# A hybrid decoder step: head sums and gate products on parts of the TensorE array, inverses on partitions 0 to 63

## The chip, the cores and the metric

The kernel runs on one core of a Trainium2 chip. The metric is the device time of one execution in microseconds (us). The core's engines work side by side, each through its own instructions in order: TensorE (PE, with its weight loads PEld), VectorE (DVE), ScalarE (ACT), GpSimd (POOL) and SyncE (SP). SP and POOL issue the DMAs here. On-chip memory has 128 partitions; matrix products go to eight PSUM banks.

## What is computed

One inference step of one decoder layer, in float32, for a new sequence of 1024 tokens and for 8 running sequences with 4 tokens each ("sampled rows", 32 in all). Two branches read the same projection `z = x @ w_in`; they are gated, merged, projected and followed by a SwiGLU network. What the change touches lies in the two branches:

```python
# RWKV-7 branch
w = -softplus(-(w0 + tanh(w_lo) @ w2)) - 0.5 ; decay = exp(-exp(w))   # w_lo: 64 columns
a = sigmoid(a0 + a_lo @ a2)                                           # a_lo: 64 columns
kk = k * k_k                                                          # 16 heads of 64 channels
kk = kk / max(sqrt(sum(kk * kk, over the head)), 1e-12)
# scan over tokens, state S (64 x 64) for each head
sa = S @ -kk ; S = S * decay + sa (x) (kk * a) + v (x) k ; y = S @ r
# RG-LRU branch: u is a causal convolution of width 4; 16 blocks of 64 channels
r = sigmoid(u_block @ wa_block + ba) ; i = sigmoid(u_block @ wi_block + bi)
a = exp(-8 * r * softplus(-lam)) ; h_t = a * h_(t-1) + sqrt(1 - a*a) * i * u
```

## The kernel before, in words

**Two parts.** The first, some 1300 us, is the mixing part: the projections of `x` and both branches. The second is the output projection's rest, the layer norms and the SwiGLU network, mostly dense products. The change touches the first, and prices that the planner uses in both.

**Tiling.** Channels lie on partitions, tokens along the free dimension. The 1024 channels are 8 tiles of 128, which is two heads each; a unit `u` is a pair of tiles (`i` = 0, 1) in one half of the sequence (`p`): 4 pairs x 2 halves = 8 units, so 16 channel tiles in all. A row of a tile is 576 columns (`W`): for p = 0 the sampled rows at 28 to 60 (`SO` to `ZO`) and 512 tokens from 64 (`PO`); for p = 1 the tokens alone. A PSUM bank holds 512 float32 columns, so `pieces(p)` cuts p = 0 into 292 and 256 columns and leaves p = 1 whole at 512.

**Projections.** `gemm_tile`, called by the main task, multiplies each weight tile with `x` as three fp32r products (high and low parts). They are recorded at line 246.

**Background tasks.** All else runs in Python generators that issue into a list; the recorded line of their instructions is 316, and matmuls of one task are told apart by tile names. A planner (`Ticker`, with a `Clock` that prices each instruction) decides the whole order before the kernel is built: between two projection matmuls it takes the first instruction of a background task that would be ready by its clock, lower `prio` first. A matmul of a task is taken once its inputs are 0.6 us old by that clock. The order on every engine is then fixed; at run time each instruction waits until its inputs are really there. `Clock.cost` holds durations, `Clock.op` what order adds: for PE 0.094 us where the part of the array changes.

**The RWKV branch.** For each tile, `wkv_tile` computes:

- the two gates with `bg_mm`, which takes a PSUM bank of the three in `Bk`, runs its list of matmuls and hands the bank to ACT. The weights `w2` and `a2` have 64 rows each; `lora` stores them over 128 rows, the other half zero, and `wa` holds `w_lo` and `a_lo` on partitions 0 to 63 and 64 to 127. Each gate is three fp32r products (`parts3`);
- the head sums: `sel` (128 x 128, two columns used) times the squares in `t6`, a float32 product, of which two rows are copied by ACT and written by four small DMAs to `ssd` in DRAM, from where `wkv` reads them as `n2`.

`stage` then copies two groups of four 64-token chunks (`g` = 0, 1) into `arm` and `bk`, and `inverse(u, g, n2)` inverts triangular matrices: float32 products of `bk` and `arm` on row halves of the array; a DMA through DRAM to `bn`; a loop of 15 steps with two small DVE instructions each on `bn`, `bt` and `btmp`, on partitions `64 * g` to `64 * g + 63`; DMAs through `bte`, `bze` and DRAM into `tdv` and `zt`; then small products on 32 x 32 quarters that DVE and ACT instructions on `zt`, `tdv` and `nz` join. `chain` carries the state over the 8 chunks of a unit: product `cx`, copies to `xs`, product `cu`, copies to `su`, product `cs_`, four updates on DVE. Each copy is made in two halves, one by ACT and one by DVE.

**The RG-LRU branch.** `lru` (lowest priority) computes the convolution `ut`, then each gate as one float32 product with a 128 x 128 weight that holds two 64 x 64 blocks on its diagonal, then activations, a scan and the products.

**Sampled rows.** `sample` handles them for p = 0. Its state update `ps2` is a pair of float32 products on two 64 x 64 quarters of the array, one from each row half, into one bank.

Of the kernel before, what the change touches and what calls it, by code (L numbers as in the profile page):

```python
# [37 lines left out]
C_ID, C_MP, C_SCAN, C_MS, C_MX, C_MB, C_SEL, C_BONES, C_M16, C_N = 0, 128, 256, 768, 832, 896, 904, 1032, 1160, 1161  # L38
# [38 lines left out]
class Clock:  # L77
# [6 lines left out]
    def __init__(self):  # L84
        self.t = dict.fromkeys(("PE", "ACT", "DVE", "POOL", "SP", "DMA"), 0.0)
        self.uses = {}
        self.masks = {}
        self.table = 0
        self.tile = None
        self.port = {"DVE": [], "POOL": []}  # L90
# [86 lines left out]
    def op(self, e, f, args, kw, at, last):  # L177
# [8 lines left out]
        else:  # L186
            if e == "PE":
# [4 lines left out]
                self.tile = tile  # L192
            lock = False
# [152 lines left out]
def tile_hybrid_step(ctx: ExitStack, tc: tile.TileContext, I, O):  # L346
# [131 lines left out]
    with ExitStack() as zctx:  # L478
# [69 lines left out]
        lora = [T(f"lora{i}", [128, 2, 2, 128], F32R) for i in range(2)]  # L548
# [41 lines left out]
        sel = cst[:, C_SEL:C_SEL + 128]  # L590
# [10 lines left out]
        for x in lora:  # L601
            pool.memset(x.bitcast(F32), 0.0)
# [89 lines left out]
        def load2(dst, src, flag, after):  # L692
# [5 lines left out]
            if len(dst[0].shape) == 3:  # L698
                split2([x.rearrange("p i m -> p (i m)") for x in dst], t[:, 0:256])
            else:  # L700
                for n in range(2):
                    b = slice(64 * n, 64 * n + 64)
                    split2([x[b, n].rearrange("p i m -> p (i m)") for x in dst], t[b, 0:256])
# [4 lines left out]
        def bg_mm(p, ops, use):  # L708

            for t0, t1 in pieces(p):  # L710
# [5 lines left out]
                Bk.put(ps)  # L716
            yield
# [10 lines left out]
        def wkv_tile(u, i, parts, side):  # L728
# [13 lines left out]
            t4 = yield from temps.take()  # L742
            yield from bg_mm(p, parts3([x[:, 1, i] for x in lora], wa),
                             lambda a, b, ps: A(t4[:, a:b], ps[:, :b - a], AF.Tanh, 0.5, D(D_A0H, q)))
# [1216 lines left out]
```

## Time and profile before

| | us |
|---|---|
| median of three runs | 2140.77 (2139.39 to 2144.16) |
| the profiled execution | 2158.58 |
| its span, first to last instruction | 2156.8 |
| mean granted TensorE clock | 0.962 |

The span is divided by the profile into busy time of each engine; a group of instructions is named by line, engine, operation and "written tile<-read tiles", with rows*columns of the array that a matmul uses, then the moving operand's shape. A float32 product is recorded as two matmuls. `bank` is any PSUM bank, `tmp` any of the 15 rows of scratch. PE's lengths include the way to PSUM, so neighbours overlap, and the distance from start to start tells what one costs.

### The profile page before, as it was taken

What the parts mean: (1) busy time and instruction counts of PE and PEld (TensorE: products, weight loads), DVE (VectorE), ACT (ScalarE), POOL (GpSimd) and SP (SyncE); (2) the same over time, 40 slices, a digit from 0 to 9 for tenths busy, and PEclk for the clock granted to TensorE, in tenths of its full rate; (3) what the DMA queues carried; (4) which work ended last, traced back from release to release, by engine and by line L of the source; (5) the groups of instructions that cost most, each with busy time, mean ns of one, the idle gap of its engine ahead of it and who ended that gap; (6) DMA issues with size and microseconds to landing.
All of it is one profiled execution on the core that took longest, in us unless ns stands there. A gap on an engine that the chain in (4) does not pass through costs nothing.

```text
span 2156.8 us, 44027 instructions
## 1 busy us (share of the span) xinstructions
PE 2065.4 (96%) x17664; PEld 1792.2 (83%) x17664; DVE 1226.6 (57%) x2967; ACT 1070.5 (50%) x2475; POOL 389.2 (18%) x797
## 2 busy tenths in 40 slices
PE   7799999999999999999999899999999999999997
PEld 7788898897986777777777697889999999999987
DVE  5676695796877887777867666522322322222226
ACT  4656756757666677767576735821121122112221
POOL 1101210220310310211212020221211211111124
PEclk9897997999999999999999799999999999999999
DMA  4131231131241231232313323221111211111112
GB/s 137 56 92 36 66 95 48 51 107 51 76 131 60 78 97 52 67 86 67 98 58 90 113 96 133 88 69 38 61 40 35 64 40 47 37 54 49 40 50 81
DMA packets 124925, 152.85 MB, mean 71 GB/s; under 512 B 82784, under 2 KB 87296, under 8 KB 124720
## 3 DMA queue, kind: packets, MB, share of 16 engines
q0 software_dynamic: 31936, 112.75, 15.6%
q1 hardware_dynamic: 92784, 37.28, 7.0%
q8 instruction: 139, 2.28, 0.4%
q14 instruction: 66, 0.54, 0.1%
HBM read 132.45 MB, written 17.57 MB: 70 GB/s over the span
## 4 chain that ended last, share of the span: by engine, by line
PE 76%; DVE 10%; ACT 9%; issue 3%; DMA 1%; POOL 0%; SPq 0%; DVEq 0%; ACTq 0%; POOLq 0%
PE bank L246 60%; PE bank L316 15%; DVE tmp L316 2%; DVE wl L316 1%; ACT tmp L316 1%; ACT wh L316 1%; DVE su L316 1%; ACT L316 1%; ACT arm L316 1%; ACT nz L316 1%; ACT bk L316 1%; DVE btmp L316 1%; DVE bt L316 1%; DVE arm L316 1%; DVE rge L316 1%
## 5 line engine op out<-in xcount | busy, mean ns | idle before, releaser
L246 PE MATMUL bank<-xx,wh 128*128 128x512 f32 (+4 forms) x3168 | 808.3, 342 | 26.9 <-ACT xx L246 8.5
L246 PEld LDWEIGHTS bank<-xx,wh 128*128 128x128 f32 x3168 | 553.5, 196 | 88.7 <-ACT xx L246 8.5
L246 PE MATMUL bank<-xx,wl 128*128 128x512 f32 (+4 forms) x1584 | 541.3, 342 | 0.0
L316 DVE TENSOR_TENSOR wl<-wraw,wh 128x512 fp32r<-128x512 f32 (+2 forms) x336 | 264.3, 788 | 264.2 <-ACT wh L316 262.1
L316 ACT ACTIVATE wh<-wraw 128x512 fp32r<-128x512 f32 (+2 forms) x408 | 246.1, 610 | 274.6 <-PE bank L246 245.6
L246 PE MATMUL bank<-hl,wh 128*128 128x272 f32 (+1 forms) x1056 | 342.6, 324 | 0.9 <-DVE hl L316 0.9
L246 PE MATMUL bank<-hh,wh 128*128 128x272 f32 (+1 forms) x1056 | 341.1, 323 | 0.5 <-ACT hh L316 0.5
L246 PE MATMUL bank<-hh,wl 128*128 128x272 f32 (+1 forms) x1056 | 341.5, 323 | 0.0
L246 PEld LDWEIGHTS bank<-xx,wl 128*128 128x128 f32 x1584 | 310.6, 196 | 28.3 <-issue 3.0
L246 PEld LDWEIGHTS bank<-hh,wh 128*128 128x128 f32 x1056 | 198.7, 188 | 17.3 <-ACT hh L316 1.2
L246 PEld LDWEIGHTS bank<-hl,wh 128*128 128x128 f32 x1056 | 198.7, 188 | 17.2 <-DVE hl L316 1.5
L246 PEld LDWEIGHTS bank<-hh,wl 128*128 128x128 f32 x1056 | 198.6, 188 | 15.3
L316 POOL DMA_DIRECT2D wraw<-in_win x114 | 61.9, 543 | 782.8 <-DVE wl L316 469.1
L316 POOL TENSOR_TENSOR wl<-wraw,wh 128x512 fp32r<-128x512 f32 (+1 forms) x72 | 86.1, 1196 | 513.3 <-ACT wh L316 490.5
L246 PE MATMUL bank<-u,wh 128*128 128x272 f32 (+1 forms) x768 | 176.7, 324 | 0.0
L246 PEld LDWEIGHTS bank<-u,wh 128*128 128x128 f32 x768 | 128.6, 188 | 11.3
L316 DVE TENSOR_TENSOR acc<-acc,bank 128x272 f32<-128x272 f32 (+3 forms) x96 | 49.9, 519 | 148.2 <-PE bank L246 148.2
L316 ACT ACTIVATE sg<-bank 128x272 f32<-128x272 f32 (+1 forms) x66 | 30.8, 466 | 196.1 <-PE bank L246 196.0
L246 PE MATMUL bank<-u,wl 128*128 128x272 f32 (+1 forms) x384 | 124.3, 324 | 0.0
L316 DVE TENSOR_TENSOR sg<-sg,bank 128x272 f32<-128x272 f32 (+1 forms) x66 | 34.3, 520 | 156.1 <-PE bank L246 156.1
L316 ACT ACTIVATE su<-bank 64x256 f32<-64x256 f32 (+1 forms) x192 | 60.2, 337 | 64.6 <-PE bank L316 62.4
L316 ACT ACTIVATE u<-sg 128x272 fp32r<-128x272 f32 (+1 forms) x66 | 33.1, 502 | 112.1 <-DVE sg L316 112.1
(248 smaller groups left out, 3204.2 us busy)
## 6 DMA issues: line engine op xcount, KB each, us to landing
wraw<-in_win POOLq DMA_DIRECT2D x116, 512.0 KB, 3.6
wraw<-in_wgu POOLq DMA_DIRECT2D x48, 512.0 KB, 3.5
wraw<-in_wo POOLq DMA_DIRECT2D x16, 512.0 KB, 3.6
wraw<-in_wdn POOLq DMA_DIRECT2D x16, 384.0 KB, 3.4
wraw<-in_wdn POOLq DMA_DIRECT2D x16, 320.0 KB, 3.2
mgd<-yb POOLq DMA_DIRECT2D x32, 128.0 KB, 2.7
out_y<-tmp SPq DMA_DIRECT2D x8, 512.0 KB
scrN<-nz SPq DMA_DIRECT2D x64, 32.0 KB
```

Source lines behind the costliest of these rows:

```text
L246: fn(*args, **kw)
L316: fn(*args, **kw)
```

## The change

It has six parts.

1. The decay and the in-context gate of a tile go side by side: `lora` now has 64 rows of each weight without zeros, and the new `pair_mm` takes two banks and issues the two gates' matmuls alternately, one on rows 0 to 63 of the array, one on rows 64 to 127. `load2` splits the weights in one instruction for all partitions, and the start of the kernel no longer clears `lora`.
2. The two gates of the RG-LRU branch: four products of 64 x 64 blocks, on four quarters of the array. Two quarters need `u` on the other half of the partitions, which two DMAs from SBUF to SBUF write into `b`, the tile that later receives the gate. The weights are stored without the zero blocks.
3. The head sums: the 512 token columns are cut into four of 128, each a product with 32 columns of `sel` on its own strip of 32 array columns and into its own 32 partitions. One copy by ACT of 128 columns takes the place of one or two of up to 512. Still four DMAs, now of two chunks each.
4. `bn`, `bt`, `btmp`, `n2` have 64 partitions and a buffer for each `g`; `bte` and `bze` have 64 partitions and serve both.
5. In `chain`, DVE now copies the lower halves and ACT the upper ones, and the four state updates go head by head.
6. The planner: prices for the new products, and 0.12 us where an ACT or DVE instruction starts at another partition than the one before it.

```diff
@@ Clock.cost, Clock.op
             if args[1].dtype == F32R:
-                return max(0.11, n / 2250)
+                return max(0.11, n / 2250) / (128 // k)
             if k <= 32:
-                return 0.045
+                return 0.045 if n == 32 else 0.024 if k == 32 else 0.017
+            if m < 128 and n > 96:
+
+                return n / 600 / min(4, 128 // k * (128 // m))
...
+            if e in ("ACT", "DVE"):
+
+                part = out.offset // out.ap[0][0]
+                at = max(at, self.t[e] + 0.12 * (self.part.get(e, part) != part))
+                self.part[e] = part
@@ tiles
-        lora = [T(f"lora{i}", [128, 2, 2, 128], F32R) for i in range(2)]
+        lora = [T(f"lora{i}", [128, 2, 128], F32R) for i in range(2)]
...
-        bn, bt, btmp = T("bn", [128, 16, 16]), T("bt", [128, 16, 16]), T("btmp", [128, 64])
-        bte, bze = T("bte", [128, 16, 32]), T("bze", [128, 16, 32])
-        n2s = [T(f"n2_{i}", [128, 16]) for i in range(2)]
+        bns, bts, btmps = [[T(f"{n}{g}", [64, *d]) for g in range(2)]
+                           for n, d in (("bn", (16, 16)), ("bt", (16, 16)), ("btmp", (64,)))]
+        bte, bze = T("bte", [64, 16, 32]), T("bze", [64, 16, 32])
+        n2s = [T(f"n2_{i}", [64, 2, 16]) for i in range(2)]
@@ new
+        def pair_mm(p, ops, use_a, use_b):
+
+
+            for t0, t1 in pieces(p):
+                while len(Bk.free) < 2:
+                    yield
+                pa, pb = Bk.get(), Bk.get()
+                for n, group in enumerate(zip(*ops)):
+                    for ps, (lhsT, rhs, *out) in zip((pa, pb), group):
+                        for w, x, o in ((lhsT, rhs, slice(0, 128)),) if not out else zip(lhsT, rhs, out[0]):
+                            MM(ps[o, :t1 - t0], w, x[:, t0:t1], start=n == 0, stop=n == len(ops[0]) - 1)
+                yield
+                use_a(t0, t1, pa)
+                Bk.put(pa)
+                use_b(t0, t1, pb)
+                Bk.put(pb)
+            yield
@@ wkv_tile
-            yield from bg_mm(p, parts3([x[:, 0, i] for x in lora], wa),
-                             lambda a, b, ps: A(t1[:, a:b], ps[:, :b - a], AF.Tanh, 0.5, D(D_W0H, q)))
+            t4 = yield from temps.take()
+            yield from pair_mm(p, [[(a[s, i], b[s]) for a, b in parts3(lora, wa)] for s in (slice(0, 64), slice(64, 128))],
+                               lambda a, b, ps: A(t1[:, a:b], ps[:, :b - a], AF.Tanh, 0.5, D(D_W0H, q)),
+                               lambda a, b, ps: A(t4[:, a:b], ps[:, :b - a], AF.Tanh, 0.5, D(D_A0H, q)))
...
-            yield from bg_mm(p, [(sel, t6)], lambda a, b, ps: A(t6[0:2, a:b], ps[0:2, :b - a]))
...
+            ps = yield from Bk.take()
+            for x in range(4):
+                MM(ps[32 * x:32 * x + 32, 0:128], sel, t6[:, PO + 128 * x:PO + 128 * x + 128], start=True, stop=True)
+            if p == 0:
+                MM(ps[0:32, 128:160], sel, t6[:, SO:ZO], start=True, stop=True)
+            yield
+            A(t6[:, PO:PO + 128], ps[:, 0:128])
+            if p == 0:
+                A(t6[0:32, SO:ZO], ps[0:32, 128:160])
+            Bk.put(ps)
+            for x in range(4):
+                g, c = x // 2, 2 * (x % 2)
+                sp.dma_start(ssd[g, i, c:c + 2].rearrange("c (h f) t -> h c (f t)", h=2),
+                             t6[32 * x:32 * x + 2, PO:PO + 128].rearrange("h (c m) -> h c m", c=2))
@@ inverse
-            pt = slice(64 * g, 64 * g + 64)
+            bn, bt, btmp, n2 = bns[g], bts[g], btmps[g], n2[:, g]
...
@@ chain
-                A(xs[0:64, :, 0], cx[0:64])
-                TC(xs[64:128, :, 1], cx[64:128])
+                TC(xs[0:64, :, 0], cx[0:64])
+                A(xs[64:128, :, 1], cx[64:128])
...
-                A(su[0:64, :, 1, 0], cu[0:64])
-                TC(su[64:128, :, 1, 1], cu[64:128])
+                TC(su[0:64, :, 1, 0], cu[0:64])
+                A(su[64:128, :, 1, 1], cu[64:128])
...
-                for i in range(2):
-                    for h in range(2):
+                for h in range(2):
+                    for i in range(2):
                         hb = slice(64 * h, 64 * h + 64)
                         to = sn[hb, i, 0, h] if c < 7 else sst[hb, 2 * pr + i]
                         STT(to, su[hb, i, 0, h], pc[hb, i, c:c + 1], cs_[hb, i], OP.mult, OP.add)
@@ lru
-                yield from bg_mm(p, [(lw[:, i, 0], ut)],
-                                 lambda a, b, ps: A(m[:, a:b], ps[:, :b - a], AF.Tanh, 0.5, D(D_BAH, q)))
                 b = yield from temps.take()
-                yield from bg_mm(p, [(lw[:, i, 1], ut)],
-                                 lambda a, c, ps: A(b[:, a:c], ps[:, :c - a], AF.Tanh, 0.5, D(D_BIH, q)))
+                lo, hi = slice(0, 64), slice(64, 128)
+                sp.dma_start(b[lo, sl], ut[hi, sl])
+                sp.dma_start(b[hi, sl], ut[lo, sl])
+                yield
+                yield from pair_mm(p, [[((lw[lo, i, 0], lw[hi, i, 0]), (ut[lo], ut[hi]), (lo, hi))],
+                                       [((lw[hi, i, 1], lw[lo, i, 1]), (b[hi], b[lo]), (lo, hi))]],
+                                   lambda a, c, ps: A(m[:, a:c], ps[:, :c - a], AF.Tanh, 0.5, D(D_BAH, q)),
+                                   lambda a, c, ps: A(b[:, a:c], ps[:, :c - a], AF.Tanh, 0.5, D(D_BIH, q)))
```

More of the change, by code (lines that the diff above doesn't have):

```diff
@@ L89, in __init__ @@
         self.tile = None
+        self.part = {}
         self.port = {"DVE": [], "POOL": []}
@@ L589, in tile_hybrid_step @@
         maskB = cst[:, C_MB:C_MB + 8]
-        sel = cst[:, C_SEL:C_SEL + 128]
+        sel = cst[:, C_SEL:C_SEL + 32]
         bones = cst[:, C_BONES:C_BONES + 128]
@@ L600, in tile_hybrid_step @@
             pool.memset(x, 0.0)
-        for x in lora:
-            pool.memset(x.bitcast(F32), 0.0)
         sp.dma_start(h0s, I["h0"])
@@ L697, in load2 @@
             sp.dma_start(t[:, 0:256], src)
[L698 to L703, printed above, removed]
+            split2([x.rearrange("p i m -> p (i m)") for x in dst], t[:, 0:256])
             temps.put(t)
@@ L754, in wkv_tile @@
             A(t5[:, sl], t4[:, sl], AF.Identity, D(D_KAH, q), D(D_KAQ, q))
-            yield from bg_mm(p, [(sel, t6)], lambda a, b, ps: A(t6[0:2, a:b], ps[0:2, :b - a]))
-            for f in range(2):
-                for g in range(2):
-                    sp.dma_start(ssd[g, i, :, f::2].rearrange("c h t -> h c t"),
-                                 t6[0:2, PO + 256 * g:PO + 256 * g + 256].rearrange("h (c f t) -> f h c t", f=2, t=32)[f])
+            ps = yield from Bk.take()
[12 more added lines that the diff above has]
+                             t6[32 * x:32 * x + 2, PO:PO + 128].rearrange("h (c m) -> h c m", c=2))
             if p == 0:
@@ L905, in inverse @@
                 yield
-            pool.memset(bt[pt], 0.0)
-            pool.memset(bt[pt].rearrange("p t j -> p (t j)")[:, 0:256:17], 1.0)
+            pool.memset(bt, 0.0)
+            pool.memset(bt.rearrange("p t j -> p (t j)")[:, 0:256:17], 1.0)
             for i in range(2):
@@ L912, in inverse @@
                 yield
-            TT(bn[pt], bn[pt], n2[pt, None, :].to_broadcast([64, 16, 16]), OP.mult)
+            TT(bn, bn, n2[:, None, :].to_broadcast([64, 16, 16]), OP.mult)
             for s in range(15):
                 m = 15 - s
-                tmp = btmp[pt, 0:m * (s + 1)].rearrange("p (t j) -> p t j", j=s + 1)
-                TT(tmp, bn[pt, s, s + 1:16].rearrange("p (t o) -> p t o", o=1).to_broadcast([64, m, s + 1]),
-                   bt[pt, s:s + 1, 0:s + 1].to_broadcast([64, m, s + 1]), OP.mult)
-                TT(bt[pt, s + 1:16, 0:s + 1], bt[pt, s + 1:16, 0:s + 1], tmp, OP.add)
+                tmp = btmp[:, 0:m * (s + 1)].rearrange("p (t j) -> p t j", j=s + 1)
+                TT(tmp, bn[:, s, s + 1:16].rearrange("p (t o) -> p t o", o=1).to_broadcast([64, m, s + 1]),
+                   bt[:, s:s + 1, 0:s + 1].to_broadcast([64, m, s + 1]), OP.mult)
+                TT(bt[:, s + 1:16, 0:s + 1], bt[:, s + 1:16, 0:s + 1], tmp, OP.add)
             for x in range(2):
-                b, d = slice(64 * g + 32 * x, 64 * g + 32 * x + 32), slice(16 * x, 16 * x + 16)
+                b, d = slice(32 * x, 32 * x + 32), slice(16 * x, 16 * x + 16)
                 TT(bte[b, :, d], bt[b], n2[b, None, :].to_broadcast([32, 16, 16]), OP.mult)
@@ L1473, in main_xb @@
             lwt = temp_wait()
[L1474 to L1475 removed]
+            sp.dma_start(lwt[:, 0:256], I["lruw"][pr].rearrange("p i s m -> p (i s m)"))
+            lw = lwt[:, 0:256].rearrange("p (i s m) -> p i s m", i=2, s=2)
             xps = []
@@ L1910, in _layout @@
     d["g2"] = pairs(g("g2_gate"))
-    lw = np.zeros((4, 128, 2, 2, 128), np.float32)
+    lw = np.zeros((4, 128, 2, 2, 64), np.float32)
     for n, nm in enumerate(("lru_wa", "lru_wi")):
@@ L1914, in _layout @@
         for h in range(2):
-            s = slice(64 * h, 64 * h + 64)
-            lw[:, s, :, n, s] = w[:, :, h].transpose(0, 2, 1, 3)
+            r = 64 * (h ^ n)
+            lw[:, r:r + 64, :, n] = w[:, :, h].transpose(0, 2, 1, 3)
     d["lruw"] = lw
```

13 lines of the change are left out of this document (4 added, 9 removed).

## The prediction

> **What bounds the kernel now.** I read the page first (busy time, then the chain that ended last), then the windows that split the span where the mixing part ends, then what waits inside that part.
>
> ```profile
> span 2156.8 us, 44027 instructions
> PE 2065.4 (96%) x17664; PEld 1792.2 (83%) x17664; DVE 1226.6 (57%) x2967; ACT 1070.5 (50%) x2475; POOL 389.2 (18%) x797
> PE 76%; DVE 10%; ACT 9%; issue 3%; DMA 1%; POOL 0%; SPq 0%; DVEq 0%; ACTq 0%; POOLq 0%
> ```
> ```profile
> 0.00:1312.00 1312.00, 1234.03 (x12524) 1042.25 (x12525) 947.38 (x2483) 852.12 (x2025) 224.17 (x617) 0.94 0.27 80
> 1312.00:2157.00 845.00, 831.41 (x5142) 749.97 (x5140) 279.18 (x485) 218.35 (x450) 164.99 (x180) 0.99 0.17 56
> ```
>
> The columns of a window are its length, then busy time (and instructions) of PE, PEld, DVE, ACT and POOL, then granted clock, DMA share and GB/s. PE bounds both parts. All that the change touches lies in the first 1312 us, where PE is busy for 1234 and stands for 78. There the main task's projections (L246) keep PE filled, and everything else (L316) is slipped between them. So PE time that goes there comes off the end, unless a new wait takes its place. The clock column says that such waits cost twice: 0.94 on average, against 0.99 later. One place shows it best.
>
> ```profile
> who waited for it (us, times):
>   PEld bank L316: 18.7, 9
>   PE bank L316: 18.5, 9
> ```
> ```profile
> 650.85 1.06 PE L316 MATMUL bank<-tdv,nz 32*32 32x32 f32 x32 [3.63 <-DVE zt L316]
> ```
> ```profile
> 643.00:650.60 7.60, 3.72 (x106) 2.94 (x106) 7.09 (x20) 0.00 (x0) 0.53 (x1) 1.00 0.22 77
> 650.80:657.40 6.60, 6.55 (x75) 5.10 (x76) 6.13 (x21) 3.19 (x7) 0.00 (x0) 0.50 0.01 2
> ```
>
> The first is the view of tile `zt`: PE waited for it nine times, 18.5 us. The second is one of these: DVE had work for 7.09 of 7.6 us, PE's next matmul stood 3.63 us behind it in PE's own order, and in the 6.6 us that follow the granted clock was 0.50.
>
> **The change part by part: matmuls.** Columns of the timeline: start, length, engine, line, operation, tiles, shape, count. Lengths overlap, so one matmul's price is the distance of starts.
>
> ```profile
> 773.32 0.84 PE L316 MATMUL bank<-wa,lora 128*128 128x512 f32 x3
> 774.00 0.62 PE L246 MATMUL bank<-xx,wh 128*128 128x512 f32 x2
> ```
> ```profile
> 57.68 0.57 PE L316 MATMUL bank<-wa,lora 128*128 128x292 f32 x3
> 58.09 0.60 PE L316 MATMUL bank<-tmp,cst 128*128 128x256 f32 x2
> ```
> ```profile
> 732.62 1.02 PE L316 MATMUL bank<-tmp,cst 128*128 128x512 f32 x2
> 733.08 0.80 PE L246 MATMUL bank<-xx,wl 128*128 128x512 f32 x1
> 733.72 0.62 PE L246 MATMUL bank<-xx,wh 128*128 128x512 f32 x2
> ```
>
> Three fp32r matmuls of 512 columns take 774.00-773.32 = 0.68 us, 0.23 each; three of 292 take 0.41, 0.137 each; by columns, 256 take 0.12. A float32 matmul stands as two records. The head sums of 512 columns run from 732.62 to 733.72 with one projection matmul of 0.23 among them: 0.87, so 0.43 a record; by columns 0.245 for 292 and 0.215 for 256.
>
> Does PE work in parts of the array side by side, and what does going there and back cost? Two kinds of such visits in before:
>
> ```profile
> 229.43 0.70 PE L316 MATMUL bank<-tmp 128*128 128x256 f32 x2
> 230.05 1.08 PE L316 MATMUL bank<-tmp,tmp 64*64 64x512 f32 x4
> 231.06 0.39 PE L246 MATMUL bank<-xx,wl 128*128 128x256 f32 x1
> 231.28 0.28 PE L246 MATMUL bank<-xx,wh 128*128 128x256 f32 x1
> ```
> ```profile
> 755.91 0.62 PE L246 MATMUL bank<-xx,wh 128*128 128x512 f32 x2
> 756.46 1.26 PE L316 MATMUL bank<-arm,bk 64*128 64x128 f32 x16
> 757.65 1.12 PE L316 MATMUL bank<-tmp 128*128 128x512 f32 x2
> 758.21 0.79 PE L246 MATMUL bank<-xx,wl 128*128 128x512 f32 x1
> 758.84 0.40 PE L246 MATMUL bank<-xx,wh 128*128 128x512 f32 x1
> ```
>
> The sampled rows' state update is two float32 products on two 64x64 quarters, four records. One after the other that is 4 x 0.43 = 1.72 us; they took 231.06-230.05 = 1.01, so two quarters run at once (0.86), with 0.15 on top; the next matmul of 256 columns took 0.22 instead of 0.12 (+0.10), and before the visit two records of 0.215 took 0.62, 0.19 too long, of which I count half. A visit costs 0.35 us beyond its streams. The second visit, row halves, 16 records of 128 columns (0.107): 0.86 in pairs; 757.65-756.46 = 1.19, before it 755.91 to 756.46 = 0.55 for two of 0.23 (+0.09), after it 758.84-757.65 = 1.19 for 0.86 + 0.23 (+0.10): 0.52 beyond the streams. These are the two bounds. I take 0.35, since the gates' visits have 512 columns like the first, under which the next weights load. No row shows four parts at once; I take it that two pairs of quarters and four strips of 32 columns also run together, and keep "only two" as a rival.
>
> Per channel tile (16: eight of the first half, p = 0, in pieces of 292 and 256 columns, eight of the second in one piece of 512):
>
> - Decay and in-context gates, six fp32r matmuls per piece, now three pairs on row halves. 512: 6 x 0.23 = 1.38 to 0.69 + 0.35 = 1.04, -0.34. 292: 0.82 to 0.41 + 0.35, -0.06. 256: 0.71 to 0.70, -0.01. Sum 8 x 0.34 + 8 x 0.07 = **-3.3 us**.
> - Recurrent branch's gates, two float32 products, now four quarters. 512: 1.72 to 0.86 + 0.35, -0.51. 292: 0.98 to 0.84, -0.14. 256: 0.86 to 0.78, -0.08. Sum 8 x 0.51 + 8 x 0.22 = **-5.8 us**.
> - Head sums, now four of 128 columns on four column strips. 512: 0.86 to 0.21 + 0.35, -0.30. First half: 0.92 to 0.21 + 0.05 (the 32 sampled columns) + 0.35, -0.31. Sum **-4.9 us**.
>
> Together -14.0 us: 64 visits (24 + 24 + 16) at 0.35 are 22.4, the streams saved are 36.4. At 0.52 a visit it is 36.4 - 33.3 = -3.1 us.
>
> A rule speaks against the recurrent gates: the Trainium skill, "TensorEngine Tiling (Array Packing)", Gotcha 1: PSUM Pressure, says that different row tiles cannot access the same PSUM bank simultaneously, and here quarters of both row halves write one bank, so two of the four would have to wait. The trace disagrees for two: the state update's quarters lie in both row halves, write one bank (`ps2`), and took 1.01 us where 1.72 would be one after the other. By the rule the sum would be that of the first rival.
>
> **DVE, ACT and the order.** The inverses move to partitions 0 to 63, and chain steps go half by half.
>
> ```profile
> 876.07 0.69 DVE L316 TENSOR_TENSOR arm<-bank,cst 64x512 f32<-64x512 f32 x1
> 876.78 0.42 DVE L316 TENSOR_TENSOR rb<-bank,cst 64x256 f32<-64x256 f32 x1
> 877.12 0.67 DVE L316 TENSOR_TENSOR arm<-bank,cst 64x512 f32<-64x512 f32 x1
> 877.81 0.43 DVE L316 TENSOR_TENSOR rb<-bank,cst 64x256 f32<-64x256 f32 x1
> ```
> ```profile
> L316 DVE SCALAR_TENSOR_TENSOR su<-su,pc,bank 64x64 f32<-64x64 f32 x224 | 62.6, 280 | 40.6 <-PE bank L316 35.9
> ```
>
> By the code, `arm` and `rb` here alternate between start partitions 64, 0, 0, 64. From rb to arm (both at 0) the next starts 0.34 us after an instruction of 0.42; where the start changes, 0.71 and 0.69 after ones of 0.69 and 0.67. So a change costs about 0.1. The chain's four state updates change start before each, now two times less: 64 steps x 0.2 = 13 us of DVE, which the other projections on PE hide, since DVE is busy 947 of 1312; if that cover is gone it is PE's waits for DVE. There I count something: before each of the nine waits for `zt`, an estimate of four changes saved, 9 x 0.4 = **-3.6 us** (bounds: 0, and all 18.5). Below nothing is possible too: the planner's prices are changed, so all instructions get another order, and waits can come as well as go. The smaller head-sum copy (128 columns for 512), the LoRA split in one instruction for two, reciprocals on twice the columns and `bte`, `bze` shared by both inverses I cost at nothing, hidden under PE.
>
> The recurrent gates add two copies between SBUF partitions, 128 to 137 KB each, ahead of their matmuls. Queued behind each on SP are the inverse's own copies; behind the matmul, in PE's order, everything.
>
> ```profile
> mgd<-yb POOLq DMA_DIRECT2D x32, 128.0 KB, 2.7
> ```
> ```profile
>   DMA zt<-scrZ: 3.4, 3
> ```
> ```profile
> 478.42 0.69 PE L316 MATMUL bank<-zt,p 32*32 32x16 f32 x62 [1.73 <-DMA zt<-scrZ]
> ```
> ```profile
> 479.90:483.30 3.40, 3.40 (x33) 2.99 (x33) 3.15 (x15) 2.60 (x5) 0.00 (x0) 0.50 0.18 43
> ```
>
> A copy of 128 KB landed after 2.7 us. The 16 copies to `zt` are the nearest case of PE behind a copy: three made it wait, 3.4 us in all. 16 recurrent gates, the same: **+3.4 us** (bounds: 0, and each as the longest, below).
>
> Sum -14.0 - 3.6 + 3.4 = -14.2 us. The profiled execution took 2158.6 us (span 2156.8 and 1.8 around it), 17.8 more than the median of the runs; it goes to 2144.4, and the median of 2140.8 to **2126.6 us**.
>
> **The rivals.**
>
> 1. *Parts run only two at a time, or a visit costs 0.52.* For it: no row shows four parts at work. Against: pairs work in both directions. The recurrent gates then take 0.86 us longer at 512 and 0.92 in the first half (14.2 in all), the head sums 0.21 (3.4): 2144. At 0.52 a visit, 2137.5. I say 2141: no change.
> 2. *A transfer takes the place of the matmuls: slower.* The gates' copies come late, since SP issues in order and shares the DMA engines with the weight loads. As at 478.42, a late one costs 1.73 us and then 3.4 us at a clock of 0.50, 1.7 more: 3.4. From the sixth late one of 16 on the gain is gone; with eight late it is 8 x 3.4 - 14.2 - 3.4 (already counted) = +10: 2150, with all 2178. For it: three of 16 in the nearest case. Against: the recurrent branch is in no hurry, so its matmuls can be placed late. The Trainium skill, "TensorE: Matmul & The Clock Gate", Part 1, has the clock halve only after an idle window of about 3.4 us; the row above shows 0.50 behind a wait of 1.73 us, so the trace disagrees.
> 3. *DVE's lateness goes.* With starts priced in the planner, PE waits half as often for `zt`: 9 us, and three stretches at half clock like the 6.6 us above go (3.3 each): -19 in place of -3.6, and 2111.
>
> **How the numbers follow.** The forecast 0.47, the first rival 0.22, the second 0.17, the third 0.14. What a measurement of this kernel can tell from no change is about 0.2%, 4.3 us. Faster: 0.44 of the forecast's, 0.04 of the first rival, all of the third: 0.62. Same: 0.03 + 0.15 + 0.01 = 0.19. Slower: 0.03 of the first, 0.16 of the second: 0.19. The forecast's own range is 2115 to 2137 (visits at 0.52; half of the third rival's gain). With the others it reaches from 2107 to 2150, where the second rival's half lies.
>
> **What would show it.** `bank<-wa,lora` should stand as 64*128 in pairs three slots long; the gates as 64*64 with eight records of 512 columns in about 1.0 us (1.9 if the first rival holds); `bank<-tmp,cst` as 128*32 in about 0.3. Waits "DMA tmp<-tmp" before the gates' matmuls would show the second rival; waits for DVE `zt` under 10 us and a clock over 0.95 in the first 1300 us the third. I am wrong if those waits grow, or if the mixing part does not end about 14 us earlier while its matmuls shrink as said.

## The result: slower by 0.8%, and the profile after

| | kernel before | changed kernel |
|---|---|---|
| median of four runs each, same chip (us) | 2141.66 (2139.39 to 2144.16) | 2159.76 (2159.64 to 2163.92) |
| ratio | 1 | 1.0081, 95% interval 1.0057 to 1.0106 |
| span of the profiled execution (us) | 2156.8, later again 2145.8 | 2157.9 |

The forecast was 14.2 us less; it is 18.1 us more, 32 us apart and outside the range that was given. The changed kernel ran in this first series only. In the later ones, partly on other chips, the median of the kernel before lay at 2144.5 to 2149.0 us; beside those the changed kernel would be 11 to 15 us slower. So comparisons below with the changed kernel carry several us of uncertainty. The first profile of the kernel before lay 17 us above its own median, so sums below go against the second profile of it (first experiment), whose execution agrees with the median of its series (2147.42).

The first lines of the page of the changed kernel, and its first window. Behind it again lie 845 us, and 5141 of PE's matmuls for 5142 in the kernel before, so it ends at the same work.

```profile
span 2157.9 us, 44476 instructions
PE 2062.7 (96%) x17856; PEld 1760.5 (82%) x17856; DVE 1188.0 (55%) x2959; ACT 1071.4 (50%) x2465; POOL 388.2 (18%) x795
```
```profile
0.00:1313.00 1313.00, 1231.20 (x12715) 1010.55 (x12716) 908.72 (x2475) 853.40 (x2015) 222.32 (x615) 0.95 0.28 83
```

The same window of the kernel before, second profile:

```profile
0.00:1300.00 1300.00, 1222.23 (x12522) 1030.74 (x12523) 947.31 (x2482) 851.25 (x2025) 224.01 (x617) 0.95 0.28 81
```

Of the changed kernel's groups by line and form, the chain's state updates (62.6 us in the kernel before):

```profile
L325 DVE SCALAR_TENSOR_TENSOR su<-su,pc,bank 64x64 f32<-64x64 f32 x224 | 53.7, 278 | 54.6 <-PE bank L325 46.7 <-ACT tmp L325 3.8 <-ACT rge L325 1.7
```

The mixing part ends 13 us later, not 14 earlier. DVE has 39 us less to do in it (8.9 of them in the state updates), and the part is longer all the same. PE is busy for 9 us more and stands for 82 instead of 78. So two questions: why did PE's work not shrink, and which waits are new?

**Where they stand together, the matmuls are as forecast.** From the timeline of the changed kernel: a whole visit of the recurrent gates, and one of the head sums (columns as before; the distance of starts is the price).

```profile
140.14 0.72 PE L325 MATMUL bank<-tmp 64*64 64x292 f32 x8
140.80 0.40 PE L255 MATMUL bank<-xx,wl 128*128 128x300 f32 x1
...
688.10 0.43 PE L325 MATMUL bank<-tmp,cst 128*32 128x128 f32 x8
688.46 0.50 PE L255 MATMUL bank<-xx,wh 128*128 128x512 f32 x1
```

Eight records of 292 columns take 0.66 us. One after the other they would take eight times 0.245: all four quarters work at once, from both row halves and two of them into each bank. The first rival falls with this, and so does, for this case, the rule of the Trainium skill beside the forecast ("TensorEngine Tiling (Array Packing)", Gotcha 1: PSUM Pressure), by which, as the prediction read it, two would have had to wait. By the code the two row halves write different partitions of the bank; no run here has them write the same ones. The head sums' eight records take 0.36 with 0.21 of stream. A LoRA visit of 512 columns, where it is whole:

```profile
765.30 0.96 PE L325 MATMUL bank<-wa,lora 64*128 64x512 f32 x6
766.20 0.50 PE L255 MATMUL bank<-xx,wh 128*128 128x512 f32 x1
```

It takes 0.90. These distances leave out what a visit costs its neighbours, which the forecast's 0.35 holds too (0.15 within the visit, 0.20 around it). Over their streams the three visits take 0.17, 0.15 and 0.21 us: the price within a visit was about right.

**But many visits come in pieces.** The same kernel, one 512-column visit of the gates, and one step of the chain's state product `cs_`:

```profile
803.22 1.08 PE L325 MATMUL bank<-tmp 64*64 64x512 f32 x4
804.23 0.50 PE L255 MATMUL bank<-xx,wh 128*128 128x512 f32 x1
...
806.97 1.08 PE L325 MATMUL bank<-tmp 64*64 64x512 f32 x4
807.97 0.50 PE L255 MATMUL bank<-xx,wl 128*128 128x512 f32 x1
...
821.72 0.45 PE L325 MATMUL bank<-su,bkt 128*64 128x64 f32 x4
822.10 0.73 PE L255 MATMUL bank<-xx,wh 128*128 128x512 f32 x2
...
823.22 0.45 PE L325 MATMUL bank<-su,bkt 128*64 128x64 f32 x4
823.59 0.50 PE L255 MATMUL bank<-xx,wh 128*128 128x512 f32 x1
```

The first two of the four quarters take 1.01 us; 2.7 us later the other two take 1.00. Half a chain product takes 0.38 and the other half 0.37. Counted in PE's order: of the 64 chain products 34 are torn (none in the kernel before), of the 24 recurrent visits 13, of the 24 LoRA visits 9 (some of them in three pieces: the 24 stand in 37). The planner takes each matmul when its own input is ready by its clock. The lower half of `su` now comes from DVE and is ready earlier than ACT's upper half; `ut` is there before its copied half. So the first half of a visit goes alone.

**The waits changed too.** In the view of tile `zt` PE now waits for it twice:

```profile
  PE bank L325: 3.6, 2
```

These were 18.5 us in nine waits, of which three (3.4 us) were for the copy to `zt` and six (15.0 us) for DVE; in the second profile of the kernel before DVE's are seven, 13.9 us. Now one is DVE's, 1.7 us: the third rival's mechanism is there. Others came. Of PE's waits in the changed kernel the two largest that are new in size, and those for `zt`; the same row for `rge` had 4.4 us in the kernel before, the one for ACT's `su` 2.2:

```profile
PE bank L255 <- DVE rge L325: 14.6, 4, 7.8
PE bank L325 <- ACT su L325: 9.6, 9, 4.0
PE bank L325 <- DMA zt<-scrZ: 1.9, 1, 1.9
PE bank L325 <- DVE zt L325: 1.7, 1, 1.7
```
```profile
888.00:896.20 8.20, 0.44 (x10) 0.28 (x6) 2.68 (x7) 7.83 (x22) 0.00 (x0) 0.50 0.26 41
896.20:904.00 7.80, 7.80 (x35) 6.05 (x35) 7.69 (x16) 2.71 (x5) 1.73 (x7) 0.69 0.00 1
```

The longest stands in the first of these windows: ACT works for 7.83 of 8.2 us, through copies of `stage` that the planner put ahead of the evacuation to `rge`, and the projection on PE has no free bank until that is done. The clock is 0.50 there and 0.69 in the next 7.8 us; it was 0.53 in the 8 us before already, so this wait did not begin the slow stretch. No PE wait of this profile is put down to the new copies to `b`.

### The profile page after: what moved, and what is told of

It reads as the page before. It is cut to its first block, busy times and chain, and to the rows that moved or that the text cites. A ratio compares the mean times of both kernels' runs of the same rounds, so it can differ in the third digit from the quotient of the medians.

```text
span 2157.9 us, 44476 instructions
## 1 busy us (share of the span) xinstructions
PE 2062.7 (96%) x17856; PEld 1760.5 (82%) x17856; DVE 1188.0 (55%) x2959; ACT 1071.4 (50%) x2465; POOL 388.2 (18%) x795
## 4 chain that ended last, share of the span: by engine, by line
PE 62%; ACT 5%; DVE 3%; issue 1%; DMA 0%; DVEq 0%; ACTq 0%; SPq 0%
PE bank L255 52%; PE bank L325 9%; DVE tmp L325 1%; ACT tmp L325 1%; ACT wh L325 1%; ACT accB L325 0%; ACT L325 0%; DVE su L325 0%; ACT bk L325 0%; ACT arm L325 0%; DVE wl L325 0%; ACT su L325 0%; DVE yb L325 0%; ACT bkh L325 0%; DVE st L325 0%
## 5 line engine op out<-in xcount | busy, mean ns | idle before, releaser
L255 PE MATMUL bank<-xx,wh 128*128 128x512 f32 (+4 forms) x3168 | 796.2, 338 | 34.2 <-DVE rge L325 14.6
L255 PEld LDWEIGHTS bank<-xx,wh 128*128 128x128 f32 x3168 | 542.2, 193 | 101.7 <-issue 12.6
L255 PE MATMUL bank<-xx,wl 128*128 128x512 f32 (+4 forms) x1584 | 531.7, 336 | 0.0
L255 PEld LDWEIGHTS bank<-xx,wl 128*128 128x128 f32 x1584 | 305.0, 193 | 33.6 <-issue 9.4
L325 ACT ACTIVATE su<-bank 64x256 f32<-64x256 f32 (+1 forms) x192 | 65.7, 342 | 66.9 <-DVE su L325 60.2
```

Of the source, the lines that this page charges most:

```text
L255: fn(*args, **kw)
L325: fn(*args, **kw)
```

## The experiments

For every trace I made one account of PE, from start to start of its matmuls: idle (nothing in flight), lost to the clock (what the granted clock lacked, times the length) and work (the rest, at full clock). It is mine, worked out from all records, good to a few us: the two profiles of the kernel before differ by 6 in work and 17 in clock. In us; the time is the ratio to the kernel before on the same chip, with its 95% interval:

| run | idle | clock | work | ratio |
|---|---|---|---|---|
| kernel before, second profile | 70.4 | 54.4 | 1999.9 | 1.0000 (0.9974 to 1.0026) |
| changed kernel | 75.3 | 54.9 | 2007.5 | 1.0081 (1.0057 to 1.0106) |
| gates, second bank first | 92.1 | 55.6 | 1999.4 | 1.0140 (1.0090 to 1.0190) |
| chain, upper half first | 103.7 | 66.6 | 2003.1 | 1.0224 (1.0183 to 1.0265) |
| both | 109.7 | 63.7 | 1980.0 | 1.0129 (1.0095 to 1.0163) |
| before + price | 75.4 | 61.3 | 2000.9 | 1.0081 (1.0054 to 1.0108) |
| before, `SPARE` 0.61 | 93.5 | 72.3 | 2000.0 | 1.0209 (1.0179 to 1.0238) |
| before, `SPARE` 0.59 | 77.8 | 43.9 | 2000.2 | 1.0027 (1.0006 to 1.0047) |
| changed - price | 84.5 | 79.9 | 2006.0 | 1.0217 (1.0186 to 1.0248) |
| changed, old recurrent gates | 74.8 | 49.8 | 2008.5 | 1.0060 (1.0032 to 1.0088) |
| before, half the gate columns | 67.9 | 62.6 | 1984.9 | 0.9959 (0.9942 to 0.9977) |
| before, all visits held | 91.6 | 58.2 | 1986.0 | 1.0049 (1.0027 to 1.0071) |
| changed, all visits held | 89.0 | 53.8 | 1973.0 | 0.9968 (0.9949 to 0.9987) |
| changed, chain held | 78.0 | 52.2 | 1997.2 | 1.0020 (0.9988 to 1.0053) |
| changed, gates held | 80.2 | 52.2 | 1995.3 | 1.0013 (0.9982 to 1.0043) |
| changed, both held | 83.6 | 55.5 | 1985.7 | 0.9991 (0.9964 to 1.0018) |
| changed, old chain copies, gates held | 83.8 | 57.3 | 1981.6 | 0.9990 (0.9961 to 1.0019) |
| changed, old chain copies, all held | 93.1 | 54.2 | 1969.8 | 0.9957 (0.9931 to 0.9984) |
| changed, old recurrent gates, all held | 84.2 | 57.3 | 1979.2 | 0.9951 (0.9927 to 0.9975) |

**1. Making visits whole through the planner.** In the first kernel the second bank's matmuls of `pair_mm`, whose input is ready last, are issued first; in the second the upper half, ACT's, of the chain's last two products; the third has both. The kernel before ran beside them.

```diff
-                    for ps, (lhsT, rhs, *out) in zip((pa, pb), group):
+                    for ps, (lhsT, rhs, *out) in reversed(list(zip((pa, pb), group))):
...
-                for h in range(2):
+                for h in (1, 0):
```

> The kernel before once more, for a second profile of it. The profiled execution of before took 2158.6 us where its runs took 2141, so the two profiles in hand differ by 1 us of span and the runs by 18. Theory 'torn visits' (PE has more work after the change): a second profile has the same PE work as the first, 1994 us at full clock, and a span near 2140, since less is lost to half clock than the 167 us at half clock of the first. Rival 'clock and waits' (the change made PE wait or run at half clock more often): the second profile shows the same 167 us at half clock and 71 us of idle PE.

> After, with the two banks of the paired gates in the other order: the matmuls whose inputs or bank come last are issued first, so that the others of the pair are ready too and the visit stays whole. Theory 'torn visits': of 24 visits of the recurrent gates 20 are whole (after: 11), of 24 of the LoRA gates 19 (after: 15); PE saves 7 to 10 us against after, so 2150 to 2153. Rival 'late copies' (PE waits for the copies between partitions): all four quarters now wait for the copies, 2160 or more. Rival 'clock and waits': no change beyond 5 us either way, 2155 to 2165.

> After, with the products cu and cs_ of the chain issued for the upper half first, whose copy ACT makes and which comes last in the plan. Theory 'torn visits': the 34 torn cs_ products of 64 become whole; su,bkt took 31.7 us of PE in after and 22.2 in before, so 9.5 us are saved: 2150. Rival 'clock and waits': no change beyond 5 us, 2155 to 2165.

> Both orders at once. Theory 'torn visits': both savings, 17 to 20 us, so 2140 to 2143, as fast as before. Rival 'clock and waits': no change beyond 5 us, 2155 to 2165.

All three were slower than the changed kernel or no better (2176.52, 2195.91 and 2176.77 us), so the theory of torn visits, as it was put there, fell. Yet more visits did become whole: with both edits 19 of the 24 LoRA visits are (15 in the changed kernel), and no half of a chain product stands alone. The work of PE did fall, by 20 against the kernel before. What grew were waits; from PE's waits in that run:

```profile
PE bank L255 <- DVE rge L325: 16.7, 3, 9.7
PE bank L325 <- ACT tmp L325: 13.1, 7, 8.8
PE bank L255 <- ACT tmp L325: 7.8, 1, 7.8
```

The edit changes when the planner finds a task ready, and with it the whole order. These runs changed two things at once.

**2. The order by itself.** The kernel before with the change's price for a new start partition and nothing else; a placebo, the kernel before with `SPARE` at 0.61 for 0.60, which no computation depends on; the changed kernel without that price; the changed kernel with the recurrent gates as before (part 2 of the change undone). The edits of the first two:

```diff
+            if e in ("ACT", "DVE"):
+                part = out.offset // out.ap[0][0]
+                at = max(at, self.t[e] + 0.12 * (self.part.get(e, part) != part))
+                self.part[e] = part
...
-    SPARE = 0.6
+    SPARE = 0.61
```

> Before, with one thing of the change: the planner's 0.12 us for an ACT or DVE instruction that starts at another partition. No instruction is other than in before, only their order. New theory 'order': what costs time is the order that the planner makes, since PE loses 130 to 170 us of the mixing part to waits and half clock, and this depends on the order alone. Then this kernel is slower than before by 10 to 30 us (by the planner's own clock its order ends 47 us later than before's). Rival 'PE work' (time follows the work of PE): PE has the same work as before, so 2147 within 5.

> A placebo: before with the planner's margin SPARE at 0.61 us for 0.60, that is the same instructions in a slightly different order, without any reason to be better or worse. Theory 'order' says that the constants of before are a lucky draw: 2155 to 2170 (by the planner's own clock this order ends 21 us later). If the order did not matter, 2147 within 5.

> After without that price; all else of the change stays. Theory 'order': the waits and the half clock go back to those of before (125 to 142 us together) and the saving of PE shows in part: 2135 to 2148. Rival 'PE work': the torn visits stay as they are in kind, so PE's work stays near 2000 us and the time at 2155 to 2165.

> After with the recurrent gates as before (two products of 128 x 128 each tile, no copies between partitions), the rest of the change kept. If the quarters and their copies cost the 13 us: 2145 to 2150. Theory 'order': the price of the planner is still there and decides, 2155 to 2175.

2159.04, 2187.12, 2187.26 and 2157.39 us. PE's work is 2000 in both variants of the kernel before; idle and clock make the difference. The placebo's largest waits:

```profile
PE bank L316 <- DVE su L316: 15.9, 17, 1.8
PE bank L316 <- DVE zt L316: 14.3, 7, 5.2
PE bank L316 <- DVE rb L316: 10.4, 7, 4.2
```

So another order alone cost these two 17 and 45 us by the ratios. But the price was no cause that could be named: without it the changed kernel became slower by another 1.4%, where 2135 to 2148 was expected. A theory that "the price spoiled the order" falls too; any edit that the planner sees draws a new order. The first placebo lies above the 2155 to 2170 that was expected. With the recurrent gates as before, at another order again, nothing changes clear of noise (1.0060 beside 1.0081), so the quarters and their copies are not by themselves what made the changed kernel slower.

**3. The order held fixed.** From here on the planner plans as before, and only what is emitted differs. In one kernel the recurrent gates' matmuls of the kernel before run over the left half of their columns; the right half of these gates is left out. In two others a background task's matmul on a part of the array is held until the last of those that stand together in its task, then all go: PE's order is as planned but for those few places. The fourth run is a second placebo with an order of its own, `SPARE` at 0.59.

```diff
+                    if half:
+                        c = (t1 - t0) // 2
+                        tk.do("PE", lambda *_, o=ps[:, :c], w=lhsT, x=rhs[:, t0:t0 + c], **kw: pe.engine.matmul(o, w, x, **kw), "matmul",
+                              (ps[:, :t1 - t0], lhsT, rhs[:, t0:t1]), dict(start=True, stop=True))
+                        continue
```
```diff
@@ Ticker.tick
-            fn(*args, **kw)
+            if e == "PE" and self.part_of(f, args):
+                task.held.append((fn, args, kw))
+                nxt = task.pend[0] if task.pend else (None, None)
+                if not (nxt[0] == "PE" and self.part_of(nxt[2], nxt[3])):
+                    for g, a, k in task.held:
+                        g(*a, **k)
+                    task.held = []
+            else:
+                fn(*args, **kw)
```

> The kernel before in its own order, instruction for instruction; only the recurrent gates' float32 matmuls run over the left half of their columns (the planner still prices the whole ones, and the right half of those gates is left out of the computation). Full, they are 28.5 us of PE by the prediction's rows (8 x (1.72 + 0.98 + 0.86)), so 14.2 us of PE go, the whole gain that was forecast, and no order changes. Theory A, order and torn visits: PE time that goes at a fixed order comes off the end nearly in full: 10 to 15 us below the kernel before. Theory B, absorbed: PE's work is not what sets the end, since the projections wait for banks and the chain's steps stay as long: at most 4 us below it, and PE's idle time grows by some 10 us.

> The changed kernel in its own planned order, with one thing moved: a matmul on a part of the array that the planner issued ahead of others of the same step is held until the last of them, so each visit is whole (64 of 64 chain products in fours, all LoRA pairs in sixes, gates in fours). Torn visits cost 9.5 us in the chain products and about 0.35 each in some 13 recurrent and 9 LoRA visits, 8 us: PE work at full clock should fall by 15 to 20 us against the changed kernel's 2007.5. Theory A: the time falls by 12 to 20 us, to about the kernel before (ratio 0.995 to 1.003). Theory B: PE work falls but the time stays within 5 us of the changed kernel (ratio about 1.007).

> The same holding of parts in the kernel before. There the chain products stand in fours already; what is torn is some of the output products and the first products of the chain (about 40 of 282 visits). Theory A: 5 to 14 us of PE work go and the time falls by 4 to 12 us. Theory B: no change, or slower by up to 10 us, as held products make the chain's steps later.

> A second placebo: the kernel before with the planner's SPARE at 0.59 for 0.60, so nothing but the order of the instructions differs. With 0.61 it was 43 us slower. Both theories: if the order alone is worth tens of us, this too differs from the kernel before by over 8 us, more likely slower (2150 to 2190). Theory A reads that as the kernel before standing on a good order, which any change to the planner's prices gives up. If it stays within 4 us, the 43 us of 0.61 were an exception, and order is no sufficient answer.

2137.30, 2138.84, 2158.93 and 2151.18 us, beside 2147.24 for the kernel before.

Half the gate columns: work falls by 15.0 (14.2 expected), the time by 8.8 (0.41% of 2147; 5 to 12 by the interval). PE time that goes does come off the end, at some six tenths of its length (0.3 to 0.8 by the interval). That is between the two theories, nearer to the first. Idle time did not grow (67.9 for 70.4); in the account the rest went to the clock (62.6 for 54.4), but two profiles of one kernel differ by more than that.

The changed kernel with all visits held is 21 us below the changed kernel (1.1% by the ratios, 0.8 to 1.4) and below the kernel before: work falls by 34.5, idle grows by 13.7. Its gates and its chain, from the timeline (held matmuls are recorded at line 334):

```profile
787.48 1.09 PE L334 MATMUL bank<-tmp 64*64 64x512 f32 x8
788.50 0.50 PE L256 MATMUL bank<-xx,wl 128*128 128x512 f32 x1
...
803.48 0.46 PE L334 MATMUL bank<-su,bkt 128*64 128x64 f32 x8
803.87 0.51 PE L256 MATMUL bank<-xx,wh 128*128 128x512 f32 x1
```

Four quarters take 1.02 us, where two alone had taken 1.00; a whole chain product 0.39, where a half had taken 0.38. These two torn visits were paid twice in full.

That is the best case. Of the eight 512-column visits of the gates in this kernel only three have all four quarters start together, one of them at a clock of 0.50 (1.90 us). In the other five the second pair comes 0.26 to 1.56 us after the first, in two of them because a copy to `b` lands then; the profile shows little of it as a wait, since the first pair keeps PE busy. One of the two:

```profile
793.68 1.07 PE L334 MATMUL bank<-tmp 64*64 64x512 f32 x4
795.24 1.08 PE L334 MATMUL bank<-tmp 64*64 64x512 f32 x4 [0.48 <-DMA tmp<-tmp]
```

Holding puts the matmuls of a visit next to each other; whether they run at once is up to their inputs and banks.

```profile
span 2136.6 us, 44474 instructions
PE 2027.0 (95%) x17856; PEld 1743.8 (82%) x17856; DVE 1188.0 (56%) x2959; ACT 1070.9 (50%) x2465; POOL 386.3 (18%) x795
```

PE is busy for 36 us less than in the changed kernel, with the same instructions on PE, DVE and ACT.

Holding isn't free: in the kernel before, whose chain visits were whole already, it takes 13.9 us of work away and adds 21 of idle time, and the time grows by 10. Two rows of PE's waits there:

```profile
PE bank L325 <- DVE su L328: 19.7, 22, 2.3
PE bank L328 <- ACT bkh L328: 5.5, 9, 1.2
```

In the second profile of the kernel before these were 8.2 us in 13 waits and 2.3 in 4:

```profile
PE bank L316 <- DVE su L316: 8.2, 13, 1.5
PE bank L316 <- ACT bkh L316: 2.3, 4, 1.1
```

The second placebo is slower by 0.27%, 6 us by the ratio and 4 by the medians, where over 8 us had been expected if order alone is worth tens of us, and under 4 if the first placebo was an exception. So it decides little: in the three variants of the kernel before that compute the same with the same instructions the order is worth 6, 17 and 45 us, and one of two placebos shows tens.

**4. Which visits.** The changed kernel at its own order with only the chain's state products held; with only the LoRA and recurrent gates held; with both; and a kernel with the chain's two copies as before (ACT the lower half) and the gates held, for which the planner makes another order and leaves all 64 chain products whole by itself. Only the test of what is held differs, and in the last one the copies:

```diff
+    def part_of(self, f, args):
+        return (f == "matmul" and args[1].tensor.name.startswith("bkt") and args[1].shape[1] == 64) or (f == "matmul" and args[1].shape[0] == 64 and self.clock.size(args[2]) >= 200)
...
-                TC(su[0:64, :, 1, 0], cu[0:64])
-                A(su[64:128, :, 1, 1], cu[64:128])
+                A(su[0:64, :, 1, 0], cu[0:64])
+                TC(su[64:128, :, 1, 1], cu[64:128])
```

> The changed kernel in its own order with the chain's state products alone held until all four of a step can go (64 whole visits for 34 torn ones); gates and everything else as the changed kernel has them. Theory C (the torn chain visits are the loss): PE work falls by about 10 us and the time by 12 to 20 us, to a ratio of 0.998 to 1.003. Theory P (the torn gates are): the time falls by 0 to 7 us only, 1.005 to 1.009. Theory S (each by its share): 7 to 12 us, 1.002 to 1.005.

> The changed kernel in its own order with the LoRA gates and the recurrent gates alone held until each visit is whole (24 whole LoRA visits for 15, all recurrent visits in fours or all their records together); the chain's torn products stay. Theory C: 0 to 7 us less, 1.005 to 1.009. Theory P: 12 to 20 us less, 0.998 to 1.003. Theory S: 7 to 12 us less, 1.002 to 1.005; PE work 8 to 12 us less.

> Both of the two holdings, and none of the others that the kernel with everything held had (the chain's other products, the output products, the inverse's quarters). Theories C, P and S alike: the sum of the two, about the time with everything held, a ratio of 0.995 to 0.999 against the kernel before; PE work near 1988. If holding the rest was what helped, it stays above 1.002.

> The changed kernel with the chain's two copies as before (ACT for the lower half, DVE for the upper), which the planner orders so that all 64 chain visits are whole by themselves, and the LoRA and recurrent gates held as in the run beside it. The planner makes a new order. If whole visits are all that counts, it comes out as the kernel with both held, 0.995 to 0.999. If the order counts as much, as the placebos say, it can lie anywhere from 0.995 to 1.015, while PE work is near 1985 all the same.

2150.86, 2151.62, 2147.89 and 2146.34 us, beside 2148.61. By the ratios each kind gives some 13 to 15 us and both together 19, each good to 8 or 9 us by the intervals. That speaks for theory S and against C and P, which each left at most 7 us to one kind, but the intervals don't exclude them, nor can it be told whether the two add up in time. In work both shares are plain, and they do add up: it falls by 10.3, 12.2 and 21.8. The torn visits counted above, 34 + 13 + 9 = 56, at the prediction's 0.35 are 19.6. That this sum is near 21.8 is partly luck: the chain's 34 would be 11.9 (10.3 measured), the gates' 22 only 7.7 (12.2 measured). A torn gate visit loses more than the coming and going, since its halves, which were to run side by side, run one after the other.

**5. Whole visits at two other orders.** The kernel with the old copies in the chain, and the changed kernel with the old recurrent gates, each with every visit held.

> The changed kernel with the chain's two copies as before (ACT the lower half, DVE the upper) and every visit held until it is whole, also the output products, the chain's first two products, the row-half products and the inverse's quarters. Against its sister with only the gates held (0.999) PE work should fall by a further 8 to 14 us. If whole visits count as at the changed kernel's own order (21 us of time for 34.5 us of PE work), it is 5 to 9 us faster than the sister: a ratio of 0.994 to 0.998. If holding the other kinds only makes waits, as in the kernel before, where 14 us of PE work less came with 21 us more of waits, it is 1.000 to 1.006.

> The changed kernel with the recurrent gates as before (two 128x128 products, no copies between partitions) and every visit held until it is whole. Against the changed kernel with everything held (0.9968) it shows what the four quarters are worth where no visit is torn: by the prediction's terms -5.8 us of PE and +3.4 us of waits for the copies, so 2 to 6 us, a ratio of 0.998 to 1.000 here. If the copies cost more than the quarters save, it is faster than 0.9968. If it lies above 1.003, the order alone is the reason, since the planner makes another one without the copies.

2137.76 and 2138.21 us, beside 2149.01: 0.43% and 0.49% faster than the kernel before. These and the changed kernel with all held beat both kernels; among the three the intervals overlap. In the first, holding the rest took 11.8 of work and some 7 us (5 to 9 was expected from the changed kernel; the kernel before had gone the other way), but the two intervals overlap, so the 7 us aren't clear of noise. The second is not slower than the changed kernel with all held: taking the four quarters out adds 6.2 of work (5.8 was the prediction's term) and takes 4.8 of idle time, at another order. In time that term is worth nothing that these runs can tell.

## Why the prediction was wrong

- **"Together -14.0 us: 64 visits (24 + 24 + 16) at 0.35."** This is the step that failed, by its number of visits: not 64 new ones but at least 120, since tearing added 56 or more. With them went a part of "the streams saved are 36.4", because the halves of a torn visit don't run side by side. Instead of falling by 14.0, PE's work rose by 7.6 (1999.9 to 2007.5). The prices of a matmul and of a whole visit were about right: with the gates' and the chain's visits held whole, PE's work is 14.2 below the kernel before (1985.7). That it meets the forecast this closely is luck, since two profiles of one kernel differ by 6 and not every held visit has its quarters run at once. I took it that a step's matmuls go out together because the code lists them together; but the planner places each for itself, by when its own input is ready. The change gave the two halves of most visits inputs from two engines, or from an engine and a DMA.
- **"The chain's four state updates change start before each, now two times less: 64 steps x 0.2 = 13 us of DVE, which the other projections on PE hide."** DVE's saving is there, 8.9 us in the state updates and 39 with the rest; no run takes it alone, so what it is worth in time isn't shown. What I left out of the same edit is what it does to PE: which half of `su` is ready first decides whether the four products of `cs_` stand together. 34 of 64 were torn, and holding them alone gave 13 us by the ratios, 10.3 of work. The prediction has no term for it.
- **"PE time that goes there comes off the end, unless a new wait takes its place."** At a fixed order it came off at about 0.6 (15.0 of work, 8.8 of time; 0.3 to 0.8 by the interval). At a new order new waits took all of it: with both kinds held, idle time is 13.2 above the kernel before against 14.2 of work less, and the ratio is 0.9991.
- **"All instructions get another order, and waits can come as well as go."** This was said, and given no size. Three other orders of the same instructions were slower by 6 to 45 us, with the kernel before the fastest of the four. The range should have been wider by this much to the slow side. With both kinds of visits held the changed kernel is level with the kernel before (0.9991, 0.9964 to 1.0018), so within that interval the tearing accounts for the whole loss against it. What kept the forecast's gain away even then is the 13.2 of idle time more; why its order has those waits I can't say beyond the single places shown.
- **DVE's waits for `zt`, -3.6.** They went from 13.9 us (15.0 in the first profile) to 1.7, so the third rival had the better size. The nine waits of the prediction counted three for the copy to `zt`, 3.4 us, as DVE's, and the next term used these three again. The waits for `rge` and `su` took the place of DVE's, so the sum of idle time gained nothing (75.3 for 70.4).
- **The copies to `b`, +3.4, and the second rival.** No PE wait is put down to them in the changed kernel, and at most 2.9 us in any other (both edits of the first experiment). They also delay the second pair of quarters, as in two of the eight visits above. Undoing quarters and copies together, at another order, made no difference clear of noise, so the changed kernel was slower by another mechanism than the rival's.
- **The first rival.** Four parts run at once where all are ready; as a limit of two it fell, with the rule beside it.
- **The planner's price** was counted at nothing by itself. Alone it cost the kernel before 17 us by the ratio; removed from the changed kernel it cost more still. That is a draw of the order and not a price.
- **The range.** Its low end, 2115, doesn't follow from "half of the third rival's gain", which gives 2119 (2126.6 less half of 15.4). The result lies beyond the other end.

## What to carry to other kernels

When work is put on parts of the array, the unit to price is the visit, and the question is whether its matmuls will be issued back to back: look at which engine or DMA each input comes from and when it is ready, and try holding the early ones until the last. It gained time at the changed kernel's order and lost time in the kernel before. When a planner makes the order, price an edit by its terms only at a fixed order; measure one or two placebos that change nothing but the order, and take their spread as the width of the forecast. PE's saved time isn't always worth its length: in the one run here that took it away at a fixed order it was worth about six tenths.

## What the runs showed of the hardware

- Two of four quarters and all four take the same time at 512 columns (1.00 and 1.02 us), from both row halves, into two banks: where all are ready together, two more cost nothing. Where the second pair came later, a visit took up to 2.6 us.
- Around a wait of 7.8 us the granted clock was 0.53 in the 8 us before, 0.50 during it and 0.69 in the 7.8 us after. In the changed kernel such stretches cost 55 us of the span, as much as in the kernel before, and 2% to 4% of the time in every run here (43.9 to 79.9 us). They don't follow the idle time of a run alone: 89.0 us idle came with 53.8, 84.5 with 79.9. What sets them off isn't shown.
- Orders of the same instructions differ by up to 2.1% in time, with work of PE equal to 1 us (1999.9, 2000.0, 2000.2 and 2000.9; the first profile of the kernel before gives 1994.3). In the slowest, idle time and clock together grew by 41 us, of 45 us of time.
